# An encoder trunk on one core: one half of an early head pair kept on chip, earlier loads of attention's output, and projections run together in twelve heads

## The chip, the core and the metric

The kernel runs on one core of a Trainium2 chip. The metric is the device time of one execution in microseconds (us); lower is better. Five engines work side by side, each through its own list of instructions: TensorE (PE, matrix products into the accumulators of PSUM), VectorE (DVE), ScalarE (ACT), GpSimd (POOL), and SyncE (SP), which issues nearly all DMA transfers. An instruction that waits holds up everything behind it on its engine.

## What is computed

A trunk of two layers on one sequence of 1024 rows and 1024 columns in float32. Layer 0 has a gMLP mixer, layer 1 chunked attention with 16 heads of 64 columns; each is followed by a gated ConvFFN. What the change touches is the attention of layer 1 with the shared K and V, cut here to its core:

```python
kv = rmsnorm(h, kv_norm_g) @ w_kv                 # k and v for all heads
q = (h @ w_q).reshape(B, nc, CHUNK, N_HEADS, HEAD_DIM) * scale
def one_chunk(args):                              # 64 rows see their chunk and 8 before
    ...
    sc = jnp.einsum('bqhd,bkhd->bhqk', qb, kb).astype(jnp.float32) + bias
    sc = jnp.where(valid[None, None, None, :], sc, NEG_INF)
    p = jax.nn.softmax(sc, axis=-1).astype(vb.dtype)
    return jnp.einsum('bhqk,bkhd->bqhd', p, vb)
...
return o @ w_o
h = h + chunk_attention(rmsnorm(h, b_norm_g[j]), k_shared, v_shared, ...)
h = h + conv_ffn(rmsnorm(h, f_norm_g[l]), ...)
```

## The kernel before

**Numbers in two parts.** Every operand of a large product is split into a high part (a cast to the fast matmul type, on ACT, L138) and a low part (the rest, mostly on DVE, L139). A product is then three matmuls: high by high, high by low and low by high (L180, L183, L187). In the names, h and l at the end tell the part: `yh`, `yl`, `whi`, `wlo`, `ph`, `pl`, `vwh`, `vwl`, `oh`, `ol`.

**Before attention** `values()` computes V in Strassen-like products (matmuls L1174, sums `c` on DVE L1136). For the weights of the last products a DVE instruction at L1118 makes `vwl`. At its end `begin("q")` and `begin("k")` load the q and k weights of head pair 1; `put_off(us, fn)` runs `fn` after so many us of matmul work have been written, so that loading, scaling (POOL) and splitting (`whi`, `wlo`) are placed between the products.

**Attention** is one loop of 128 steps, `s = 8*hd + i`: head `hd`, key block `i`. A step writes, in this order:

- `head.score(i)`: scores of up to 5 query blocks against the key block (L1414 and L1416), a near tile of 256 columns and a far one (at `i = 4` one tile of 512). DVE adds the bias (L1420), ACT takes the exponentials (far L1424, near L1421) and casts to `ph` (L1427), POOL makes `pl` (L1428).
- fill products: matmuls of the q and k projections of later pairs, `n` of them, about 5.8 a step, one half here and the other half behind the values. From step `ends` = 104 (head 13) on the fill is the output projection `wo`.
- `mx.block(b)`: row maxima of the next head, a near block `mx` (L1229, DVE L1231) and a far one (L1235, DVE L1237). At a step they stand either in the middle (`mid`) or at the end (`end`). After step 5 the maxima are transposed (`mr`, L1252), copied by ACT, and a DMA writes them as one row of `qe`, which the next head's first score needs.
- `h0.value(b)`: probabilities by V of the step two before (L1444, L1446, L1448).

The tiles `st`, `mx` and `mr` share four PSUM banks, so that a new tile may wait for the reader of an older one.

**After a pair** p (two heads) and for each half t of the rows: ACT and DVE copy the product out (L1469, L1473), the sums of the softmax go through memory and come back as `den` (L1498), and `scale` divides (L1503), splits into the one buffer `oh`, `ol`, and `store` writes both to `osave` (L1512, L1513). `stays` marks a half that isn't stored but stays on chip in a place of `new_y()`. The output projection loads the stored halves with `load_o` (L1345, L1346), two transfers of 256 KB for one half of a pair. `load_hr` loads rows of the residual (L1574), `output_weight` the weights of `wo` (L1553), and `stage` copies q and k of the next head into place (L1215).

**What sets the order.** PE's instructions run in the order in which they are written. A scheduler sets the order on the other engines, SP's queue among them, and so decides which transfer is issued first.

Of the kernel before, what the change touches and what calls it, by code (L numbers as in the profile page):

```python
# [22 lines left out]
KD = D // P  # L23
# [23 lines left out]
def trunk(ctx: ExitStack, tc: tile.TileContext, x, a_win, a_wv, a_wst, a_bs, a_wout, w_kv, w_q, w_o,  # L47
# [1215 lines left out]
    with tc.tile_pool(name="vt", bufs=3, reuse_waits="tile") as vt, tc.tile_pool(name="vx", bufs=3, reuse_waits="tile") as vx, \  # L1263
# [16 lines left out]
        for t, _ in enumerate(values()):  # L1280
# [13 lines left out]
            if t:  # L1294
                def begin(what):
                    raw = new_raw([P, KD, P])
                    nc.sync.dma_start(raw, (w_q if what == "q" else w_kv)[1])
                    put_off(7.0, lambda: gains(what, raw))

                def gains(what, raw):  # L1300
                    c = C_BG if what == "q" else C_KVG
                    G.tensor_tensor(raw, raw, cc[:, c:c + KD].unsqueeze(2).broadcast_to([P, KD, P]), op=ALU.mult)
                    put_off(4.0, lambda: parted(what, raw))

                def parted(what, raw):
                    ws = [new_w() for _ in range(2)]
                    with tc.issue_after(behind[S].ins):
                        for i in range(2):
                            split(*ws[i], raw.rearrange("p k c -> p (k c)")[:, halves[i]])
                    w1[what] = tuple(Halves(t) for t in zip(*ws))  # L1310
                put_off(9.0, lambda: begin("q"))
                put_off(21.0, lambda: begin("k"))
                put_off(8.0, first_max)
# [35 lines left out]
    with tc.tile_pool(name="b1", bufs=1, reuse_waits="tile") as b1, \  # L1349
# [103 lines left out]
        class Pair:  # L1453
# [6 lines left out]
            def done(self, c, t, po):  # L1460
# [16 lines left out]
                stays = t == 0 and p >= LAST - 1  # L1477
# [40 lines left out]
                waits = (8.0, 8.0) if stays else (8.5, 8.0) if p == LAST - 1 else (10.5, 13.5 if p == LAST - 2 and t == 0 else 9.0)  # L1518
# [50 lines left out]
        def load_hr(i):  # L1569
            place = f32(bt.tile([P, T], F32R, tag=("thi", "tlo")[i % 2], name="hr"))  # L1570
            for j in range(2):
                hr[2 * i + j] = place[:, halves[j]]
                with tc.issue_after(behind["row"].ins):
                    nc.sync.dma_start(hr[2 * i + j], hsave[1][2 * i + j, :, halves[0]])  # L1574
# [3 lines left out]
        left = 2 * 6 * KD * LAST - early  # L1578
        ends = 13 * NB
        mid, end = {1: (1,), 2: (3,), 3: (5,), 4: (7,)}, {0: (0,), 1: (2,), 2: (4,), 3: (6,)}  # L1580
        for s in range(NH * NB):
# [11 lines left out]
            if s in (ends - 3, ends - 2, ends - 1, ends):  # L1593
                for k in ((0, 1), (2,), (3,), (4,))[s - ends + 3]:
                    load_o(k, 0)
# [7 lines left out]
            if s == ends + 6:  # L1603
                load_o(LAST - 2, 0)
# [21 lines left out]
            for _ in range(n // 2):  # L1626
                next(fill, None)
# [5 lines left out]
            if len(waiting) > LAG:  # L1633
                h0, b = waiting.pop(0)
                h0.value(b)
            for _ in range(n - n // 2):
                next(fill, None)
            if mx:
# [178 lines left out]
```

## Time and profile before

| | us |
|---|---|
| median of three runs | 2129.46 (2129.17 to 2131.74) |
| profiled execution | 2133.36 |
| its span in the trace | 2131.6 |
| attention's first score | at 1047.8 |
| head 13's first score | at 1342.06 |
| head 14's first score | at 1371.52 |

Times within the execution are counted from the start of the span. A row of the timeline gives the start, the duration, the engine with its source line, output and inputs, and in brackets how long the engine had been idle and what released it. A row of the view of waits sums such idle time by what was waited for, with the number of times and the longest. A row of the view of windows gives, for a stretch, each engine's busy time, PE's granted clock (PEclk, as a share of full speed), and what the DMA engines moved.

### The profile page before, as it was taken

What the parts mean: (1) busy time and instruction counts of PE and PEld (TensorE: products, weight loads), DVE (VectorE), ACT (ScalarE), POOL (GpSimd) and SP (SyncE); (2) the same over time, 40 slices, a digit from 0 to 9 for tenths busy, and PEclk for the clock granted to TensorE, in tenths of its full rate; (3) what the DMA queues carried; (4) which work ended last, traced back from release to release, by engine and by line L of the source; (5) the groups of instructions that cost most, each with busy time, mean ns of one, the idle gap of its engine ahead of it and who ended that gap; (6) DMA issues with size and microseconds to landing.
All of it is one profiled execution on the core that took longest, in us unless ns stands there. A gap on an engine that the chain in (4) does not pass through costs nothing.

```text
span 2131.6 us, 28895 instructions
## 1 busy us (share of the span) xinstructions
PE 2106.1 (99%) x9829; PEld 1758.3 (82%) x9829; DVE 1572.0 (74%) x2343; ACT 1086.2 (51%) x1896; POOL 790.0 (37%) x566
## 2 busy tenths in 40 slices
PE   9999999999999999999999999899999999999998
PEld 7888878888888888878888888788888888888887
DVE  5287789888888857776556666665988888885576
ACT  6533555554445544553466666653545544454443
POOL 1475744332334412042466655531322423342020
PEclk9999999999999999999999999999999999999999
DMA  7667722454445966734656566761244544478653
GB/s 255 194 243 261 238 99 100 138 187 142 169 164 195 330 226 221 263 101 143 187 132 167 140 157 162 197 216 62 72 152 136 183 139 172 164 274 309 211 189 129
DMA packets 205435, 384.63 MB, mean 180 GB/s; under 512 B 44388, under 2 KB 64204, under 8 KB 205288
## 3 DMA queue, kind: packets, MB, share of 16 engines
q1 hardware_dynamic: 201480, 376.88, 54.1%
q10 hardware_dynamic: 3808, 5.91, 0.8%
q8 instruction: 77, 1.26, 0.2%
q14 instruction: 70, 0.57, 0.1%
HBM read 247.28 MB, written 113.36 MB: 169 GB/s over the span
## 4 chain that ended last, share of the span: by engine, by line
PE 87%; DVE 6%; DMA 3%; issue 1%; ACT 1%; POOL 0%; SPq 0%; ACTq 0%; DVEq 0%; POOLq 0%
PE up L1044 10%; PE gate L1044 10%; PE up L368 7%; PE up L370 7%; PE up L373 7%; PE gate L373 6%; PE gate L368 5%; PE gate L370 5%; PE vps L520 4%; PE v L1174 3%; PE qkv L180 2%; PE qkv L183 2%; PE qkv L187 2%; PE ups L180 1%; PE ups L183 1%
## 5 line engine op out<-in xcount | busy, mean ns | idle before, releaser
L139 DVE TENSOR_TENSOR wlo<-raw,whi 128x512 fp32r<-128x512 f32 x376 | 332.1, 890 | 156.7 <-ACT whi L138 156.6
L138 ACT CAST whi<-raw 128x512 fp32r<-128x512 f32 x378 | 233.7, 620 | 269.6 <-PE gate L1044 194.4
L368 PE MATMUL up<-yh,whi 128*128 128x512 f32 x688 | 268.1, 390 | 0.5 <-ACT gate L930 0.5
L370 PE MATMUL up<-yh,wlo 128*128 128x512 f32 x688 | 268.0, 389 | 0.0
L891 POOL TENSOR_TENSOR h<-a 128x512 f32<-128x512 f32 x44 | 84.9, 1929 | 402.6 <-DVE a L883 390.0
L1428 POOL TENSOR_TENSOR pl<-p,ph 128x640 fp32r<-128x640 f32 (+4 forms) x128 | 159.0, 1245 | 146.8 <-ACT ph L1427 112.8
L368 PE MATMUL gate<-th,whi 128*128 128x512 f32 x496 | 193.1, 389 | 0.0
L370 PE MATMUL gate<-th,wlo 128*128 128x512 f32 x496 | 193.1, 389 | 0.0
L373 PE MATMUL up<-yl,whi 128*128 128x512 f32 x688 | 184.2, 389 | 0.0
L368 PEld LDWEIGHTS up<-yh,whi 128*128 128x128 f32 x688 | 129.2, 188 | 28.0 <-ACT gate L930 1.2
L373 PEld LDWEIGHTS up<-yl,whi 128*128 128x128 f32 x688 | 129.2, 188 | 27.2 <-POOL yl L139 0.5
L370 PEld LDWEIGHTS up<-yh,wlo 128*128 128x128 f32 x688 | 129.2, 188 | 26.6
L139 DVE TENSOR_TENSOR yl<-raw,yh 128x512 fp32r<-128x512 f32 x172 | 142.0, 827 | 8.1 <-ACT yh L138 8.1
L373 PE MATMUL gate<-tl,whi 128*128 128x512 f32 x496 | 132.8, 390 | 0.3 <-DVE tl L139 0.3
L138 ACT CAST whi<-S 128x512 fp32r<-128x512 f32 x160 | 99.1, 619 | 66.6 <-PE up L373 60.6
L139 DVE TENSOR_TENSOR wlo<-S,whi 128x512 fp32r<-128x512 f32 x160 | 130.2, 815 | 0.0
L1044 PE MATMUL up<-yl,whi 128*128 128x512 f32 (+1 forms) x312 | 120.8, 387 | 0.1
L1044 PE MATMUL up<-yh,wlo 128*128 128x512 f32 (+1 forms) x312 | 120.5, 386 | 0.2 <-DVE wlo L139 0.2
L1044 PE MATMUL up<-yh,whi 128*128 128x512 f32 (+1 forms) x312 | 120.5, 386 | 0.0
L1044 PE MATMUL gate<-yh,wlo 128*128 128x512 f32 (+1 forms) x312 | 120.4, 386 | 0.0
L1044 PE MATMUL gate<-yh,whi 128*128 128x512 f32 (+1 forms) x312 | 120.3, 385 | 0.0
L1044 PE MATMUL gate<-yl,whi 128*128 128x512 f32 (+1 forms) x312 | 120.2, 385 | 0.0
(452 smaller groups left out, 5397.9 us busy)
## 6 DMA issues: line engine op xcount, KB each, us to landing
raw<-in_f_win SPq DMA_DIRECT2D x88, 512.0 KB
gT<-h SPq DMA_DIRECT2D x88, 256.0 KB
h<-in_f_wdown SPq DMA_DIRECT2D x44, 512.0 KB
dS<-h SPq DMA_DIRECT2D x88, 256.0 KB
raw<-dS SPq DMA_DIRECT2D x40, 512.0 KB
raw<-gT SPq DMA_DIRECT2D x40, 512.0 KB
gB<-a SPq DMA_DIRECT2D x66, 256.0 KB
raw<-in_f_wdown SPq DMA_DIRECT2D x30, 512.0 KB
```

What stands on the lines that cost most here:

```text
L138: behind[S] = S.copy(hi, src)
L139: return eng.tensor_tensor(lo, src, f32(hi), op=ALU.subtract)
L180: nc.tensor.matmul(ps, wh[:, k, :], xs[k][0], start=k == first, stop=False)
L183: nc.tensor.matmul(ps, wl[:, k, :], xs[k][0], start=False, stop=False)
L368: nc.tensor.matmul(ps, wh[:, k, :], xs[k][0], start=first and k == 0, stop=False, skip_group_check=True)
L370: nc.tensor.matmul(ps, wl[:, k, :], xs[k][0], start=False, stop=False, skip_group_check=True)
L373: nc.tensor.matmul(ps, wh[:, k, :], xs[k][1], start=False, stop=k == 3, skip_group_check=True)
L520: nc.tensor.matmul(ps, a, b, start=k == i == 0, stop=k == KD - 1 and i == 2)
L891: G.tensor_tensor(B[n], x, B.get(y) if isinstance(y, str) else y, op=ALU.subtract)
L1044: nc.tensor.matmul(ps[:, cs], w[:, ms], x[:, cs], start=q == i == 0 and p in (1, 6, 5, 4), stop=q == NP - 1 and i == 2, skip_group_check=True)
L1174: nc.tensor.matmul(bank[m], a, b, start=p not in (2, 7) and k == i == 0, stop=k == 3 and i == 2, skip_group_check=True)
L1428: marks[2] = G.tensor_tensor(pl[:, :n], pf[:, :n], f32(ph[:, :n]), op=ALU.subtract)
```

## The change

1. `begin("k")` is put off by 25 us instead of 21.
2. `stays` holds for the first half (t = 0) of pair 5 too: it isn't stored in `osave` and isn't loaded again. The waits before `turned` and `scale` are adapted.
3. The places of the five loaded halves (pairs 0 to 4) are taken at step `ends - 3`, and all loads are written at steps `ends - 3` and `ends - 2`; before they were spread over four steps.
4. `load_hr` stays behind the last load of `o` where there is one, otherwise behind the last `row` DMA.
5. In the first twelve heads (`merged`) a step has another order: score, the end blocks of `mx` held over from the step before, value, mid blocks, and then all `n` fill products in one run.

```diff
-                put_off(21.0, lambda: begin("k"))
+                put_off(25.0, lambda: begin("k"))
...
-                stays = t == 0 and p >= LAST - 1
+                stays = t == 0 and p >= LAST - 2
...
-                waits = (8.0, 8.0) if stays else (8.5, 8.0) if p == LAST - 1 else (10.5, 13.5 if p == LAST - 2 and t == 0 else 9.0)
+                waits = ((8.5, 9.0) if t else (8.0, 8.0)) if p == LAST - 1 else (10.5, 13.5 if stays else 9.0)
...
-                with tc.issue_after(behind["row"].ins):
+                with tc.issue_after(behind["o"].ins if "o" in behind else behind["row"].ins):
                     nc.sync.dma_start(hr[2 * i + j], hsave[1][2 * i + j, :, halves[0]])
...
-        left = 2 * 6 * KD * LAST - early
+        left, held = 2 * 6 * KD * LAST - early, ()
...
-                for k in ((0, 1), (2,), (3,), (4,))[s - ends + 3]:
-                    load_o(k, 0)
+                if s == ends - 3:
+                    slots = [new_y() for _ in range(5)]
+                for k in ((0, 1), (2, 3, 4), (), ())[s - ends + 3]:
+                    load_o(k, 0, at=slots[k])
...
-            if s == ends + 6:
-                load_o(LAST - 2, 0)
...
-            for _ in range(n // 2):
-                next(fill, None)
+            merged = s < 12 * NB
+            for b in held:
+                mx.block(b)
+            held = []
+
+            def value():
+                if len(waiting) > LAG:
+                    h0, b = waiting.pop(0)
+                    h0.value(b)
+            if merged:
+                value()
+            else:
+                for _ in range(n // 2):
+                    next(fill, None)
             if hd + 1 < NH:
                 for b in mid.get(i, ()):
                     mx.block(b)
...
-            if len(waiting) > LAG:
-                h0, b = waiting.pop(0)
-                h0.value(b)
-            for _ in range(n - n // 2):
+            if not merged:
+                value()
+            for _ in range(n if merged else n - n // 2):
                 next(fill, None)
-            if mx:
+            if mx and merged:
+                held = end.get(i, ())
+            elif mx:
                 for b in end.get(i, ()):
                     mx.block(b)
```

What this does to the engines' lists is shown at three places. A row is the source line, the operation, its output and inputs with the buffers' numbers, the shape, and the engines or DMA queues that the instruction waits for.

**PE, head 2, step 4**, from the step's score on. Before, three projections (`qkv`) stand between the score and block 7 of the maxima (`mx`), and the values (`po`) follow:

```order
L1414 MATMUL st_10257<-qe0_8344,km0_8346 128x512 [waits DVE_49]
L1416 MATMUL st_10257<-qs0_8345,ks0_8343 128x512
L180 MATMUL qkv_10157<-yh_8541,whi_9730 128x512
L183 MATMUL qkv_10157<-yh_8541,wlo_9731 128x512
L180 MATMUL qkv_10157<-yh_8550,whi_9730 128x512
L1229 MATMUL mx_10270<-km1_9386,qe1_9384 128x256 [waits DVE_49]
L1235 MATMUL mx_10274<-km1_9386,qe1_9384 128x384 [waits DVE_49]
L1444 MATMUL po_10194<-ph_10180,vh0_9388 128x256
L1446 MATMUL po_10194<-ph_10180,vl0_9390 128x256
L1448 MATMUL po_10194<-pl_10181,vh0_9388 128x256 [waits Pool_49]
L1444 MATMUL po_10198<-ph_10180,vh0_9388 128x384
L1446 MATMUL po_10198<-ph_10180,vl0_9390 128x384
```

and with the change, the same step:

```order
L1414 MATMUL st_10250<-qe0_8344,km0_8346 128x512 [waits Activation_49]
L1416 MATMUL st_10250<-qs0_8345,ks0_8343 128x512
L1229 MATMUL mx_10260<-km1_9386,qe1_9384 128x256 [waits DVE_49]
L1235 MATMUL mx_10264<-km1_9386,qe1_9384 128x384 [waits DVE_49]
L1444 MATMUL po_10184<-ph_10173,vh0_9388 128x256
L1446 MATMUL po_10184<-ph_10173,vl0_9390 128x256
L1448 MATMUL po_10184<-pl_10174,vh0_9388 128x256 [waits Pool_49]
L1444 MATMUL po_10188<-ph_10173,vh0_9388 128x384
L1446 MATMUL po_10188<-ph_10173,vl0_9390 128x384
L1448 MATMUL po_10188<-pl_10174,vh0_9388 128x384
L1229 MATMUL mx_10273<-km1_9386,qe1_9384 128x256 [waits DVE_49]
L1235 MATMUL mx_10277<-km1_9386,qe1_9384 128x384 [waits DVE_49,Activation_49]
```

The two blocks of the step before (first `mx` pair) now stand right behind the score, the values ahead of block 7, and the projections behind all of it; the last row waits for ACT too, since its bank held the score `st` of the same step. Of the twelve merged heads the last row waits for ACT in six (2, 4, 6, 8, 10 and 11) and for DVE alone in the others.

**DVE, in `values()`, where the k weights of pair 1 are split** (`wlo`; `vwl` is the low part of a V weight, `c` a sum of the V products). Before:

```order
L1136 TENSOR_TENSOR c_9212<-v_9195,x_8391 128x512 [waits DMAHW3_49,DVE_49]
L139 TENSOR_TENSOR wlo_9240<-raw_9107,whi_9239 128x512 [waits Activation_49]
L139 TENSOR_TENSOR wlo_9242<-raw_9107,whi_9241 128x512 [waits Activation_49]
L1118 SCALAR_TENSOR_TENSOR vwl_9187<-raw_9185,cc_68,vwh_9186 128x512 [waits DMAHW0_49,Activation_49]
L1136 TENSOR_TENSOR c_9250<-v_9225,raw_8390 128x512 [waits DMAHW4_49,DVE_49,PE_49]
L1136 TENSOR_TENSOR c_9253<-v_9225,x_8391 128x512 [waits DMAHW5_49,DVE_49]
L1118 SCALAR_TENSOR_TENSOR vwl_9217<-raw_9215,cc_68,vwh_9216 128x512 [waits DMAHW1_49,Activation_49]
```

with the change:

```order
L1118 SCALAR_TENSOR_TENSOR vwl_9187<-raw_9185,cc_68,vwh_9186 128x512 [waits DMAHW0_49,Activation_49]
L1118 SCALAR_TENSOR_TENSOR vwl_9216<-raw_9214,cc_68,vwh_9215 128x512 [waits DMAHW1_49,Activation_49]
L1136 TENSOR_TENSOR c_9242<-v_9224,raw_8390 128x512 [waits DMAHW4_49,DVE_49,PE_49]
L1136 TENSOR_TENSOR c_9245<-v_9224,x_8391 128x512 [waits DMAHW5_49,DVE_49]
L139 TENSOR_TENSOR vtl_9257<-h10_83,vth_9256 128x512 [waits Activation_49]
L1136 TENSOR_TENSOR c_9273<-v_9260,raw_8389 128x512 [waits DMAHW6_49,DVE_49,PE_49]
L139 TENSOR_TENSOR wlo_9285<-raw_9148,whi_9284 128x512 [waits Activation_49]
L139 TENSOR_TENSOR wlo_9287<-raw_9148,whi_9286 128x512 [waits Activation_49]
```

The two splits of the k weights have moved from ahead of two `vwl` to six rows behind them.

**ACT and SP, pair 5's second half.** On ACT, in head 13's first steps, the cast of that half into `oh` (`oh`, the third row; the two ahead of it are exponentials of the step's scores). Before:

```order
L1424 ACTIVATE p_13435<-st_13441,cc_68 128x384 [waits PE_49,Pool_49]
L1421 ACTIVATE p_13435<-p_13435 128x256 [waits DVE_49]
L138 CAST oh_13159<-o_12867 128x512 [waits DMAHW7_49,DVE_49]
L1427 CAST ph_13445<-p_13435 128x640 [waits Activation_49]
L1424 ACTIVATE p_13473<-st_13479,cc_68 128x384 [waits PE_49,Pool_49]
```

with the change:

```order
L1424 ACTIVATE p_13433<-st_13439,cc_68 128x384 [waits PE_49,Pool_49]
L1421 ACTIVATE p_13433<-p_13433 128x256 [waits DVE_49]
L138 CAST oh_13157<-o_12860 128x512 [waits DVE_49]
L1427 CAST ph_13443<-p_13433 128x640 [waits Activation_49]
L1424 ACTIVATE p_13471<-st_13477,cc_68 128x384 [waits PE_49,Pool_49]
```

The cast no longer waits for a DMA queue; nothing else has moved there. On SP, ahead of head 13, the last rows up to the loads of `osave` and the transfers that bring the second half's sums (`rden51`, then `den`) and head 14's q and k (`qe0`, `km0`, `qs0`, `ks0`). Before:

```order
L1498 DMA den_12726<-rden50_9363 64x512 [waits DMAHW7_49,DMAHW6_49]
L1498 DMA den_12726<-rden50_9363 64x512
L1215 DMA qs0_8345<-thi_12962 64x512 [waits DMAHW0_49]
L1215 DMA km0_8346<-thi_13282 64x512 [waits DMAHW1_49,Activation_49]
L1215 DMA qs0_8345<-tlo_12963 64x512 [waits DMAHW2_49]
L1496 DMA rden51_9365<-few_13161 128x2x4 [waits DMAHW3_49,DVE_49]
L1215 DMA ks0_8343<-thi_13282 64x512 [waits DMAHW4_49]
L1215 DMA ks0_8343<-tlo_13283 64x512 [waits DMAHW5_49,DVE_49]
L1498 DMA den_12868<-rden51_9365 64x512 [waits DMAHW6_49,DMAHW3_49]
L1498 DMA den_12868<-rden51_9365 64x512 [waits DMAHW7_49]
L1346 DMA yl_13403<-osave_9341 128x512 [waits DMAHW0_49,PE_49]
L1346 DMA yl_13430<-osave_9341 128x512 [waits DMAHW1_49,PE_49]
```

with the change:

```order
L1345 DMA yh_13313<-osave_9341 128x512 [waits DMAHW7_49]
L1346 DMA yl_13314<-osave_9341 128x512 [waits DMAHW0_49,PE_49]
L1215 DMA qe0_8344<-thi_12962 64x512 [waits DMAHW1_49]
L1215 DMA km0_8346<-thi_13280 64x512 [waits DMAHW2_49,Activation_49]
L1215 DMA qs0_8345<-thi_12962 64x512 [waits DMAHW3_49]
L1496 DMA rden51_9365<-few_13159 128x2x4 [waits DMAHW4_49,DVE_49]
L1215 DMA qs0_8345<-tlo_12963 64x512 [waits DMAHW5_49]
L1215 DMA ks0_8343<-tlo_13281 64x512 [waits DMAHW6_49,DVE_49]
L1215 DMA ks0_8343<-thi_13280 64x512 [waits DMAHW7_49]
L1259 DMA bias_13572<-in_bias 128x256 [waits DMAHW0_49,DVE_49]
L1498 DMA den_12861<-rden51_9365 64x512 [waits DMAHW4_49,DMAHW1_49]
L1498 DMA den_12861<-rden51_9365 64x512 [waits DMAHW2_49]
```

Before, two of the ten loads of `osave` stood behind the second half's `den`; now all ten stand ahead of it, and the `den` of the first half (`den_12726` before) has moved ahead of nine of them, out of the rows shown.

## Prediction, on record before the changed kernel ran

> **What bounds the kernel now.** I read the page first, then PE's waits.
>
> ```profile
> PE 2106.1 (99%) x9829; PEld 1758.3 (82%) x9829; DVE 1572.0 (74%) x2343; ACT 1086.2 (51%) x1896; POOL 790.0 (37%) x566
> PE 87%; DVE 6%; DMA 3%; issue 1%; ACT 1%; POOL 0%; SPq 0%; ACTq 0%; DVEq 0%; POOLq 0%
> ```
>
> TensorE is busy for 2106.1 us of a span of 2131.6, and the change takes no matmul away. So it can gain only from PE's 25.5 us of idle time, and from what a slower clock behind an idle stretch costs. The waits say where:
>
> ```profile
> PE st L1414 <- DVE mb L1231: 8.0, 2, 7.8
> PE v L1174 <- DVE vwl L1118: 1.9, 2, 1.0
> PE st L1414 <- DMA qe<-mr: 1.1, 3, 0.5
> PE po L1448 <- POOL pl L1428: 0.9, 1, 0.9
> PE po L1444 <- ACT ph L1427: 0.3, 1, 0.3
> ```
>
> One wait of 7.8 us stands out. The windows put it into head 13; the first row holds heads 0 to 12, the second head 13, the others are pieces of it:
>
> ```profile
> 1047.80:1342.00 294.20, 292.17 (x1586) 252.99 (x1585) 187.31 (x510) 188.55 (x397) 174.48 (x151) 1.00 0.60 152
> 1342.00:1371.50 29.50, 21.65 (x117) 19.06 (x117) 16.47 (x42) 16.46 (x36) 14.17 (x13) 0.88 0.74 219
> ...
> 1350.00:1352.00 2.00, 0.00 (x0) 0.00 (x0) 0.00 (x0) 0.00 (x0) 0.00 (x0) 0.61 0.84 257
> 1352.00:1354.00 2.00, 0.00 (x0) 0.00 (x0) 0.76 (x2) 1.72 (x4) 0.40 (x1) 0.50 0.53 132
> 1354.00:1356.00 2.00, 1.67 (x6) 1.57 (x7) 1.68 (x7) 1.75 (x5) 1.61 (x2) 0.50 0.94 291
> 1356.00:1358.00 2.00, 2.00 (x10) 1.73 (x9) 1.02 (x4) 1.48 (x3) 1.71 (x2) 0.69 0.96 247
> ```
>
> Heads 0 to 12 leave PE only 2.03 us idle in 294; head 13 leaves 7.85 in 29.5. Behind its stall the granted clock is 0.50 until about 1357.3, while PE works from 1354.34 on: 3 us at half speed, 1.5 us lost. The same windows (0.61, 0.69) put the half clock from 1350.4 to 1357.2, so it came 4 us after PE went idle. Head 13's stall is worth **9.4 us** in all.
>
> **The change, part by part.** *Pair 5's first half stays (change 2).* The stall, followed back:
>
> ```profile
> 1346.27 0.22 PE L1235 MATMUL mx<-km,qe 128*128 128x128 f32 x1
> 1354.34 0.58 PE L1414 MATMUL st<-qe,km 128*128 128x256 f32 x1 [7.85 <-DVE mb L1231]
> 1353.24 0.69 DVE L139 TENSOR_TENSOR ol<-o,oh 128x512 fp32r<-128x512 f32 x1 [7.32 <-DMA osave<-ol]
> 1352.28 0.62 ACT L138 CAST oh<-o 128x512 fp32r<-128x512 f32 x1 [7.14 <-DMA osave<-oh]
> 1344.43 0.33 SPq L1512 DMA_DIRECT2D osave<-oh x1
> 1345.56 0.67 SPq L1513 DMA_DIRECT2D osave<-ol x1
> ```
>
> The score waits for DVE's `mb`, which stands behind `ol`, which waits with ACT's `oh` for the one buffer `oh`, `ol`: the store of pair 5's first half, issued at 1344.43 and 1345.56, must have left it. With the change this store doesn't exist, and the cast waits for DVE alone. What is late next is the second half's own sums:
>
> ```profile
> 1343.71 1.07 DVE L1503 TENSOR_TENSOR o<-o,den 128x512 f32<-128x512 f32 x1 [0.66 <-DMA den<-rden]
> 1345.51 0.41 DVE L1420 TENSOR_TENSOR p<-st,bias 128x256 f32<-128x256 f32 x1
> 1353.85 0.42 DVE L1231 CUSTOM_DVE_ANT_0 junk<-mx,bias 128x256 f32<-128x256 f32 x1
> 1339.90 1.10 SPq L1498 DMA_DIRECT2D den<-rden x2
> 1341.09 1.01 SPq L1346 DMA_DIRECT2D yl<-osave x2
> 1332.00:1336.00 4.00, 4.00 (x24) 3.59 (x23) 4.00 (x9) 2.31 (x6) 1.57 (x2) 1.00 0.99 262
> 1336.00:1340.00 4.00, 4.00 (x25) 3.15 (x23) 1.59 (x3) 1.63 (x5) 2.38 (x4) 1.00 0.77 170
> ```
>
> Were `den` as early as before, DVE would be free at 1345.92, make `ol` (0.69) and `mb` (0.42), and release the score at 1347.0, 0.5 us after PE came to it at 1346.49. But the two `yl` loads that were issued behind `den` now stand ahead of it (change 3): 0.5 MB, at the 170 to 262 GB/s of these windows 2.0 to 3.1 us. `den` had 0.66 us of wait already, but part of the extra falls where the queue idled, so I take 1.2 to 2.4 us more for DVE, and a stall of 1.7 to 2.9 us that remains, 2.0 as the value. Then 5.9 us of idle time go, and 1.5 of half clock, since such a stall ends before the 4 us are over. For a wait of head 14's first maxima on `km0`, which is issued behind the same ten loads, I take 0.9 off. **Head 13: −6.5 us**; bounds −3 (a stall of some 5 us stays, with its half clock) and −9.
>
> The Trainium skill, "TensorE: Matmul & The Clock Gate", Part 1 (the HAM clock gate), has the clock fall to half after an idle window of about 3.4 us, and return after about 3.4 us of work. The trace agrees: the half clock came after 4 us of idle time and ended 3 us after work came back. By this rule a stall of 2 us costs no half clock, and the sum stays; were the clock lost in proportion to the stall, 0.4 us of the 1.5 would stay and the sum be −9.1 instead of −9.5.
>
> No longer loading that half at `ends + 6` gives PE nothing by itself, since the first use of any loaded half is at step 104 or later and no wait on `yh` or `yl` stands among PE's waits. Its split keeps its work on ACT and DVE, into another place; that place is free, as no wait is added there. Change 4 moves residual loads by a few us, which are used long after.
>
> *The end of attention.* The second half of pair 6 has the same pattern, smaller:
>
> ```profile
> 1395.55 0.69 DVE L1503 TENSOR_TENSOR o<-o,den 128x512 f32<-128x512 f32 x1 [2.32 <-DMA den<-rden]
> 1397.58 0.49 PE L1444 MATMUL po<-ph,vh 128*128 128x512 f32 x1 [0.35 <-ACT ph L1427]
> 1399.24 0.50 PE L1448 MATMUL po<-pl,vh 128*128 128x512 f32 x1 [0.93 <-POOL pl L1428]
> ```
>
> DVE waits 2.32 us for `den` with the next bias add behind it, and PE pays 0.35 and 0.93 us two steps later, with some 0.2 for each restart of its pipeline. With `waits` of (8.5, 9.0) the multiplication stands behind that bias add and its cast behind `ph`. **−1.7 us**, bounds 0 and −1.9.
>
> *The k weights (change 1).*
>
> ```profile
> 1020.72 1.28 DVE L139 TENSOR_TENSOR wlo<-raw,whi 128x512 fp32r<-128x512 f32 x2
> 1021.92 0.74 DVE L1118 SCALAR_TENSOR_TENSOR vwl<-raw,cc,vwh 128x512 fp32r<-128x512 f32 x1
> 1023.78 0.74 DVE L1118 SCALAR_TENSOR_TENSOR vwl<-raw,cc,vwh 128x512 fp32r<-128x512 f32 x1
> ```
>
> Two `wlo`, 1.28 us, stand ahead of the two `vwl` for which PE waits 1.9 us. Now both `vwl` come first, the second ahead of two `c` of 0.6 us as well. **−1.8 us**, bounds −1 and −1.9. The k weights are about 5 us later; the 48 products of q in front of their first use (0.23 us each, 11 us) cover that.
>
> *The merged steps (change 5).* The same matmuls in another order; the price is what they wait for. A step as before, head 4, step 4:
>
> ```profile
> 1149.06 0.39 PE L1414 MATMUL st<-qe,km 128*128 128x512 f32 x1
> 1149.29 0.40 PE L1416 MATMUL st<-qs,ks 128*128 128x512 f32 x1
> 1149.91 0.41 DVE L1420 TENSOR_TENSOR p<-st,bias 128x256 f32<-128x256 f32 x1
> 1150.36 0.42 ACT L1421 ACTIVATE p<-p 128x256 f32<-128x256 f32 x1 [2.24 <-DVE p L1420]
> 1150.68 0.46 ACT L1424 ACTIVATE p<-st,cc 128x256 f32<-128x256 f32 x1
> ```
>
> Here is a new wait: with the change block 7's far matmul takes the bank of this step's score in six heads, and the far exponential (L1424) must have read it. That ends at 1151.14, 1.85 us after the second score matmul began. In the merged order PE would come to it 1.5 us after that, when the other bank's two `mx` and the six values are through (0.23 for the score's rest, 0.12 and 0.18 for `mx`, 0.88 for the values, 0.12). So 0.35 us of stall, 0.4 with the restart: 2.4 us in six heads, and at 0.1 each 0.6 in the others, whose row waits for an earlier DVE instruction. Against it, the blocks of maxima no longer crowd at the end of one step and the start of the next. The 2.03 us of idle time in heads 0 to 12 bound what can be seen of this; start to start, the matmuls of heads 0 to 11 take 5.1 us more than their usual spacing, 3.8 of it at step 2, where DVE is late with a maximum every other head. I take 2.8 of the 3.8 as gained. The wait for `qe<-mr`, 1.1 us in three heads, I leave as it is: `mr` comes one product later (0.23 us), the copy on ACT that it shares the engine with comes sooner; between 0.9 lost and 1.1 gained. Values come half a step sooner, by 0.5 to 1.1 us; `pl` was ready 0.6 us or more before its first use in these heads, mostly 2 to 3, so this costs at most a few tenths. Sum 2.4 + 0.6 − 2.8 + 0.3: **+0.5 us**, bounds −4 (every gap gone, no new wait) and +6 (0.6 us in each of twelve heads, nothing gained but 1).
>
> **Sum:** −6.5 − 1.7 − 1.8 + 0.5 = −9.5 us. The profiled execution took 2133.36 us, and would take 2123.9. The median shown is 2129.46, 3.9 us below it; with the same difference, **2120.0**. If part of the stall belongs to the profiled execution alone, the gain is smaller.
>
> **The rivals.**
>
> *The transfers take the stall's place* (little gained). Ten loads in one block ahead of `den`, `km0` and the rest. For it: DMA moved 257 GB/s in the middle of the stall already (window 1350 to 1352), and SP issues in order. Against it: 1 MB of stores and loads is gone from this stretch and the next. If head 13 keeps its whole stall, −1.7 − 1.8 + 0.5 = −3: 2126.5. [...]
>
> *The new wait on the score's bank decides* (slower). Place: block 7 at step 4 of the twelve merged heads. Its price is 0.4 us where ACT is free; if ACT has a cast (0.62 us, as in the row of `oh`) or two ahead of the exponentials, it is 1.0 to 1.6, and the values of the next steps come late too. From 1.2 us in each head, 14.4 in all, it eats the 10 us gained elsewhere and 4.3 more: 2134 and above. Against it: in head 4 ACT had been idle for 2.24 us when its exponential came.
>
> *Merging costs half of that* (0.6 us in each head, 7.2 more than the sum has): 2127.
>
> *All gaps go* (much faster): head 13 −9.4, the two others −3.5, and −4 from heads 0 to 11, which gives −17: 2112.5. Against it stands `den`'s lateness.
>
> That the cast still waits for a store is ruled out by its row on ACT; the store of the first half is gone from SP.
>
> **How the numbers follow.** The sum has 0.67, its own range 2117 to 2123; the transfers in the stall's place 0.13; the bank wait as a decider 0.06; merging at half that 0.06; all gaps gone 0.08. A measurement of this kernel tells about 0.2% from no change, 4.3 us: faster is under 2125.2, slower over 2133.7. The sum and the case of all gaps are faster, and a small part of the transfers' case: 0.76. The rest of that case and of the half-priced merging is within 0.2%: 0.18. Slower is the bank wait: 0.06. The range leaves out that and most of the case of all gaps: **2115 to 2127**.
>
> **What would show it.** Right: PE's wait on `mb` in head 13 falls from 7.85 to 1.5 to 3 us, and the granted clock stays at 1.0; the two waits on `vwl` and those on `ph` and `pl` at the end are gone; the heads 0 to 11 take as long as before within 2 us, with a new wait of L1235 on ACT's far exponential at step 4. Wrong: a wait on `qe`, `km` or `den` of 5 us in head 13 or 14; heads of 23.5 us and more before it; or the half clock again.

## The result and the profile after

The changed kernel takes 2127.32 us (median of 22 runs), the kernel before, run beside it, 2130.8 us (22 runs): a ratio of **0.9983, 95% interval 0.9976 to 0.9990**, 3.5 us less. The forecast was 9.5 us less, and 2115 to 2127 us. The profiled execution took 2130.35 us, with a span of 2128.6 against 2131.6.

PE's waits in the changed kernel's profile (us in total, times, longest):

```profile
PE po L1448 <- POOL pl L1428: 2.4, 3, 1.7
PE po L1444 <- DVE o L1473: 2.2, 1, 2.2
PE mx L1229 <- DVE mb L1231: 1.4, 2, 1.1
PE mx L1229 <- DMA km<-thi: 1.4, 1, 1.4
PE st L1414 <- DVE mb L1231: 1.3, 2, 0.7
```

The 7.8 us of head 13 and the two waits on `vwl` are gone. In their place stand waits that the kernel before had not, or not so long; only the score's wait on `mb`, the last row, is in part a rest of the old one. By stage, from the first score of a head to that of another, the two profiles give:

| stage | before, us | after, us | difference | forecast |
|---|---|---|---|---|
| up to head 0's first score | 1047.87 | 1045.61 | −2.3 | −1.8 |
| heads 0 to 11 (merged) | 270.58 | 272.51 | +1.9 | +0.5 |
| head 13 | 29.46 | 24.02 | −5.4 | −6.5 |
| end of attention: steps 0 to 3 of head 15, up to their last values (L1448 at 1402.40, 1398.66) | 10.08 | 12.07 | +2.0 | −1.7 |

Heads 12 and 14 are unchanged within 0.05 us. The sum is −3.8; 0.7 us are lost elsewhere, behind these steps. The merged heads and the end of attention are furthest from their forecast. Each profile is one execution, though, and the same stages differ between executions, as the profiles of the experiments show.

**Head 13** after, first as a window, then DVE and SP at its start, then PE's three waits:

```profile
1341.70:1365.80 24.10, 20.98 (x118) 17.69 (x118) 15.21 (x41) 15.60 (x35) 13.80 (x13) 1.00 0.76 206
```

```profile
1345.42 0.69 DVE L1503 TENSOR_TENSOR o<-o,den 128x512 f32<-128x512 f32 x1 [2.75 <-DMA den<-rden]
...
1341.97 1.10 SPq L1498 DMA_DIRECT2D den<-rden x2
...
1346.98 0.38 PE L1229 MATMUL mx<-km,qe 128*128 128x256 f32 x1 [1.11 <-DVE mb L1231]
1348.26 0.39 PE L1414 MATMUL st<-qe,km 128*128 128x256 f32 x1 [0.62 <-DVE mb L1231]
1352.71 0.39 PE L1229 MATMUL mx<-km,qe 128*128 128x256 f32 x1 [1.40 <-DMA km<-thi]
```

No store is waited for any more and the clock stays at 1.00. What is left is what now comes late: `den`, for which DVE waits 2.75 us instead of 0.66, and `km` of head 14.

**The end of attention** after, on DVE, ACT, POOL and PE, and the granted clock behind it:

```profile
1390.11 2.08 DVE L1503 TENSOR_TENSOR o<-o,den 128x512 f32<-128x512 f32 x1
1390.08 1.56 POOL L1428 TENSOR_TENSOR pl<-p,ph 128x640 fp32r<-128x640 f32 x1 [0.77 <-ACT ph L1427]
1392.22 0.62 ACT L138 CAST oh<-o 128x512 fp32r<-128x512 f32 x1 [1.43 <-DVE o L1503]
1392.86 0.58 ACT L1472 COPY den<-po 64x512 f32<-64x512 f32 x1
1393.66 0.68 DVE L1473 COPY o<-po 64x512 f32<-64x512 f32 x1
1394.40 0.33 PE L1444 MATMUL po<-ph,vh 128*128 128x128 f32 x1 [2.19 <-DVE o L1473]
```

```profile
1394.00:1396.00 2.00, 1.60 (x8) 1.46 (x9) 1.73 (x2) 1.94 (x5) 1.55 (x1) 0.79 0.94 287
1396.00:1398.00 2.00, 2.00 (x8) 1.81 (x7) 1.77 (x3) 2.00 (x5) 1.56 (x1) 0.50 0.92 320
1398.00:1400.00 2.00, 2.00 (x11) 1.78 (x10) 1.04 (x2) 0.81 (x2) 1.03 (x1) 0.86 0.37 134
```

The multiplication L1503 stands later, as forecast, and no longer waits for `den`. But it now runs while POOL makes `pl`, and takes 2.08 us instead of 0.69. Behind it stand ACT's cast `oh`, DVE's `ol`, and then the copies L1472 and L1473 that free PE's bank `po`: PE waits 2.19 us for them, and the clock is at half for 3.4 us on top.

**Head 7**, a merged head. SP's order, POOL, and PE's longest wait there:

```profile
1206.38 0.39 SPq L1512 DMA_DIRECT2D osave<-oh x1
1206.87 0.38 SPq L1513 DMA_DIRECT2D osave<-ol x1
1207.35 0.43 SPq L1373 DMA_DIRECT2D vl<-vd x1
1208.48 0.35 SPq L155 DMA_DIRECT2D raw<-in_w_q x1
1216.83 1.90 POOL L158 TENSOR_TENSOR raw<-raw,cc 128x1024 f32<-128x1024 f32 x1 [4.29 <-DMA raw<-in_w_q]
1218.68 2.78 POOL L1428 TENSOR_TENSOR pl<-p,ph 128x640 fp32r<-128x640 f32 x2
1220.27 0.33 PE L1448 MATMUL po<-pl,vh 128*128 128x128 f32 x1 [1.66 <-POOL pl L1428]
```

and the same place in the kernel before:

```profile
1208.04 0.42 SPq L155 DMA_DIRECT2D raw<-in_w_q x1
1209.21 0.38 SPq L1373 DMA_DIRECT2D vl<-vd x1
1210.34 0.33 SPq L1512 DMA_DIRECT2D osave<-oh x1
1212.54 1.90 POOL L158 TENSOR_TENSOR raw<-raw,cc 128x1024 f32<-128x1024 f32 x1
```

All projections of a step now stand at its end, and so the weights for the next ones are asked for later, behind two stores of 256 KB and the load of `vl`. POOL multiplies them by the gain 8.35 us after the issue instead of 4.5, waits 4.29 us for them, and `pl` stands behind it. PE, which comes to the values sooner than before, waits for that.

### The profile page after: what moved, and what is told of

The parts are those of the page before. It is cut to its first block, busy times and chain, and to the rows that moved or that the text cites. A ratio compares the mean times of both kernels' runs of the same rounds, so it can differ in the third digit from the quotient of the medians.

```text
span 2128.6 us, 28878 instructions
## 1 busy us (share of the span) xinstructions
PE 2106.5 (99%) x9829; PEld 1759.2 (83%) x9829; DVE 1576.7 (74%) x2343; ACT 1087.6 (51%) x1896; POOL 790.5 (37%) x566
## 5 line engine op out<-in xcount | busy, mean ns | idle before, releaser
L1044 PE MATMUL up<-yl,whi 128*128 128x512 f32 (+1 forms) x312 | 120.8, 387 | 0.2
L1044 PE MATMUL up<-yh,wlo 128*128 128x512 f32 (+1 forms) x312 | 120.5, 386 | 0.2
L1044 PE MATMUL up<-yh,whi 128*128 128x512 f32 (+1 forms) x312 | 120.4, 386 | 0.0
L1044 PE MATMUL gate<-yh,wlo 128*128 128x512 f32 (+1 forms) x312 | 120.4, 386 | 0.0
L1044 PE MATMUL gate<-yh,whi 128*128 128x512 f32 (+1 forms) x312 | 120.2, 385 | 0.0
L1044 PE MATMUL gate<-yl,whi 128*128 128x512 f32 (+1 forms) x312 | 120.1, 385 | 0.0
```

The source lines that it names most:

```text
L1044: nc.tensor.matmul(ps[:, cs], w[:, ms], x[:, cs], start=q == i == 0 and p in (1, 6, 5, 4), stop=q == NP - 1 and i == 2, skip_group_check=True)
```

## The experiments

Ratios are to the kernel before, each with runs of it beside; medians are compared inside one group only (e1 to e4, e5 to e8, e9 to e12). "Heads 0 to 11" is the time from the first score of head 0 to that of head 12 in the profile.

### Without the merged steps (e1)

```diff
-            merged = s < 12 * NB
+            merged = False
```

> The change without its merged steps (part 5), all else kept. Theory A (the merged order itself costs: values come sooner and wait for POOL's pl behind its multiplication of the weights, 2.4 us of PE waits plus a half clock in head 7, against the gaps at step 2 that it removes): 2 to 4 us faster than the changed kernel, that is about 6 us (0.9970) faster than before, and in the profile heads 0 to 11 take 5 us over the usual spacing as before. Theory B (head 7's wait was an accident of the one profiled execution, a slow weight load; merging else gains): 0 to 3 us slower than the changed kernel, 0.5 to 3.5 us faster than before.

Measured: 0.9977 (0.9968 to 0.9986), 2126.99 us. Heads 0 to 11 take 270.05 us against 272.51 in the changed kernel, and no wait on `pl` stands there; the end of attention has the same 2.2 us. The gain over the changed kernel's 0.9983 lies inside the intervals, so the time alone doesn't settle it. This profile speaks for A, others in part for B. The profiles of e2, e3, e4 and e7 have the merged steps with the same order on SP in head 7, and heads 0 to 11 take 270.48, 268.83, 268.69 and 272.32 us there. PE's wait on `pl` in head 7 is 1.18 us in e2 and 2.17 in e7; in e3 and e4, where POOL waited 2.06 and 2.11 us for the weights instead of 4.29, PE doesn't wait. So what merging costs differs from one execution to the next: from 2.5 us more than in e1 to 1.4 less.

### The wait of 8.0 us for pair 6's second half (e2)

```diff
-                waits = ((8.5, 9.0) if t else (8.0, 8.0)) if p == LAST - 1 else (10.5, 13.5 if stays else 9.0)
+                waits = ((8.5, 8.0) if t else (8.0, 8.0)) if p == LAST - 1 else (10.5, 13.5 if stays else 9.0)
```

> The change with the wait of pair 6's second half put back from 9.0 to 8.0 us, so that its multiplication by the softmax sums (L1503) stands ahead of the second bias add of head 15 again. Theory A (the later place is what costs the 2.2 us wait on L1473 and the half clock behind it): that wait goes, den is there by 1388 in this kernel's time since no load of osave is under way, the stretch of head 15's steps 0 to 3 costs under 1 us, and the kernel is 3 us faster than the changed kernel, about 6.5 us faster than before. Theory B (den comes late there whatever the place, as in the kernel before): PE's waits on ph and pl of 1.3 us come back, and the kernel is at most 1.5 us faster than the changed one.

Measured: 0.9974 (0.9965 to 0.9983), 2126.69 us. DVE and PE at the end of attention:

```profile
1388.39 0.69 DVE L1503 TENSOR_TENSOR o<-o,den 128x512 f32<-128x512 f32 x1 [2.02 <-DMA den<-rden]
1392.08 0.50 PE L1448 MATMUL po<-pl,vh 128*128 128x512 f32 x1 [0.93 <-POOL pl L1428]
```

The wait on L1473 and the half clock are gone, as A says; `den` is as late as before (2.02 us, before 2.32), as B says, and 0.93 us of wait on `pl` come back. With POOL idle L1503 takes 0.69 us.

The four steps of the end of attention take 9.79 us, against 12.07 in the changed kernel. But 1.5 us of that difference is the half clock, which need not follow. Eight more kernels here have the later place (e1, e3, e4, e6, e7, e9, e10, e12), all with the same wait of 2.2 us on L1473; in seven of them no half clock follows, and the four steps take 10.51 to 10.65 us, against 10.08 before. Nor does the earlier place keep it away: in e8 the four steps take 12.17 us, with a half clock. So the later place is no gain: it costs 0.4 to 0.6 us, and 2.0 where the half clock follows it. Head 13 took 26.67 us in this profile, 2.7 more than in the changed kernel: DVE waited 4.58 us for `den` there, and 6.8 us of half clock followed.

### The loads of o spread as before (e3)

```diff
-                if s == ends - 3:
-                    slots = [new_y() for _ in range(5)]
-                for k in ((0, 1), (2, 3, 4), (), ())[s - ends + 3]:
-                    load_o(k, 0, at=slots[k])
+                for k in ((0, 1), (2,), (3,), (4,))[s - ends + 3]:
+                    load_o(k, 0)
```

> The change with the five loads of o spread over steps 101 to 104 as before; merged steps and all else kept. Theory A (the ten loads in one block delay den and km0 ahead of heads 13 and 14): the waits on mb (2.3 us) and on km (1.6 us) in head 13 fall to under 1.5 us together, and the kernel is 1.5 to 3 us faster than the changed one. Theory B (those transfers are late anyhow, or DVE's own order sets the wait on mb): head 13 keeps 3 us or more of waits, and the time is within 1 us of the changed kernel.

Measured: 0.9969 (0.9958 to 0.9980), 2125.47 us. PE's waits:

```profile
PE mx L1229 <- DMA km<-thi: 2.3, 1, 2.3
PE po L1444 <- DVE o L1473: 2.2, 1, 2.2
PE st L1414 <- DVE mb L1231: 0.6, 1, 0.6
PE mx L1229 <- DVE mb L1231: 0.3, 1, 0.3
```

In head 13 the waits on `mb` fell (one of those rows, 0.3, is head 12's), but the one on `km` grew to 2.3 us: the two theories are both half right. The stall moves between the transfers. Head 13 takes 25.60 us in this profile, with a half clock behind the wait on `km`, 1.6 more than in the changed kernel; so this profile doesn't explain the better median by head 13.

### The k weights at 21 us (e4)

```diff
-                put_off(25.0, lambda: begin("k"))
+                put_off(21.0, lambda: begin("k"))
```

> The change with the k weights begun at 21 us as before. The two waits on vwl (1.9 us) come back, with their restarts: 2 us slower than the changed kernel, 1.5 us faster than before. If the place of the k weights' split is hidden, no difference to the changed kernel.

Measured: 0.9986 (0.9976 to 0.9996), 2128.76 us. The row `vwl` is back with 1.9 us, and head 0 begins at 1046.98 instead of 1045.61. In the median the part can't be told from no difference. Head 13 has the same order here as in the changed kernel, but DVE waited 4.30 us for `den` in this execution, and PE lost a half clock behind it.

### The merged steps alone (e5)

The kernel before with the order of part 5, as in the diff of the change:

```diff
+            merged = s < 12 * NB
+            for b in held:
+                mx.block(b)
...
+            if merged:
+                value()
```

> The kernel before with the merged steps alone (part 5). Theory A (values that come sooner wait for POOL's pl, at head 3, head 5 and, where the weights come late, head 7; what is gained at step 2 is given back): heads 0 to 11 take 3 to 7 us over the usual spacing against 5 before, the profile shows waits of L1448 on pl of 1 us or more in sum, and the time is within 1.5 us of before. Theory B (merging gains the gaps of heads 0 to 11, and the changed kernel's waits came from the other parts): 2 to 4 us faster than before, no wait on pl there.

Measured: 1.0005 (0.9992 to 1.0017), 2133.94 us; the profiled execution was the slowest of its runs. Heads 0 to 11 take 273.29 us, against 270.58 before, and PE's waits have this row:

```profile
PE po L1448 <- POOL pl L1428: 3.8, 3, 2.6
```

2.6 us of it are in head 7, 0.3 in head 5, 0.9 at the end of attention. Merging alone shows no gain: the interval leaves out B's 2 to 4 us.

### Values behind half of the projections (e6)

```diff
+            for _ in range(n // 2):
+                next(fill, None)
             if merged:
                 value()
-            else:
-                for _ in range(n // 2):
-                    next(fill, None)
...
-            for _ in range(n if merged else n - n // 2):
+            for _ in range(n - n // 2):
```

> The change with the merged steps in another order: score, the held blocks, half of the projections, then values, middle blocks and the other half. Values come 0.5 to 0.7 us later than in the change. Theory A (it is the earlier values that wait for pl): the waits on pl in heads 3, 5 and 7 go or fall under 0.3 us each, the far block of step 4 no longer waits for ACT, heads 0 to 11 take under 3 us over the usual spacing, and the kernel is 2 us faster than the changed one. Theory B (POOL is late whatever the order): the waits on pl stay, no difference.

Measured: 0.9991 (0.9977 to 1.0005), 2130.06 us, which can't be told from no difference. The waits on `pl` in heads 5 and 7 and that of the far block of step 4 went, but head 3's grew:

```profile
PE po L1444 <- DVE o L1473: 3.6, 5, 2.2
PE st L1414 <- DMA qe<-mr: 2.0, 3, 0.9
PE po L1448 <- POOL pl L1428: 1.5, 1, 1.5
```

and four waits on L1473 inside the merged heads and three on `qe` came with it. Heads 0 to 11 take 273.15 us. A fails as it was put: later values alone don't help, since other waits take their place. And in head 7 it isn't the later values that helped. With half of the projections ahead of them the weight load is issued ahead of the stores again, and POOL doesn't wait for it:

```profile
1205.79 0.38 SPq L155 DMA_DIRECT2D raw<-in_w_q x1
1207.10 0.38 SPq L1373 DMA_DIRECT2D vl<-vd x1
1208.35 0.33 SPq L1512 DMA_DIRECT2D osave<-oh x1
1210.54 1.91 POOL L158 TENSOR_TENSOR raw<-raw,cc 128x1024 f32<-128x1024 f32 x1
```

That is 4.75 us from issue to multiplication, as in the kernel before: it is the load's place on SP that decides in head 7.

### The low parts behind den (e7)

```diff
-                for k in ((0, 1), (2, 3, 4), (), ())[s - ends + 3]:
-                    load_o(k, 0, at=slots[k])
+                for k in ((0, 1, 2, 3, 4), (), (), ())[s - ends + 3]:
+                    os_[0][k] = slots[k]
+                    behind["o"] = nc.sync.dma_start(f32(slots[k][0]), osave[0, k, :, halves[0]])
+                for k in ((), (), (0, 1, 2, 3, 4), ())[s - ends + 3]:
+                    behind["o"] = nc.sync.dma_start(f32(slots[k][1]), osave[1, k, :, halves[0]])
```

> The change with the five loads of the high parts of o at step ends - 3 and those of the low parts only at ends - 1, so that the second half's den stands ahead of the low parts on SP. Theory A (the loads ahead of den set the wait on mb): DVE's wait for den in head 13 falls from 2.8 to under 1.2 us, and PE's waits on mb there to 1 us or less; the transfers behind, km of head 14 or the low parts themselves, come later, so that a wait of 2 to 5 us on them is new and the time is about that of the changed kernel, within 2 us. Theory B (den is late for another reason): DVE's wait for den stays at 2 us or more.

Measured: 0.9967 (0.9953 to 0.9981), 2125.85 us. DVE's wait for `den`, and PE's wait on `km`:

```profile
1340.90 0.69 DVE L1503 TENSOR_TENSOR o<-o,den 128x512 f32<-128x512 f32 x1 [0.29 <-DMA den<-rden]
```

```profile
PE mx L1229 <- DMA km<-thi: 3.0, 1, 3.0
```

With five loads ahead of `den` instead of ten its wait falls from 2.75 to 0.29 us, and `km`, now behind the low parts, is 3.0 us late. That is theory A: it is the loads in front that decide when `den` comes. Head 13 as a whole gains nothing by it in this profile: it takes 25.12 us, with a half clock behind the wait on `km`.

### Kept half, k weights, spread loads and 8.0 us together (e8)

The edits of e1, e2 and e3 on the change:

```diff
+            merged = False
...
+                waits = ((8.5, 8.0) if t else (8.0, 8.0)) if p == LAST - 1 else (10.5, 13.5 if stays else 9.0)
...
+                for k in ((0, 1), (2,), (3,), (4,))[s - ends + 3]:
+                    load_o(k, 0)
```

> The parts that gained, together: pair 5's half kept on chip and the k weights later, without the merged steps, with the loads of o spread as before and with the wait of 8.0 us for pair 6's second half. If the gains add (e1, e2 and e3 each alone are 1.3 to 2.9 us faster than the changed kernel), 9 us faster than before, 0.9958. If they are not independent (the transfers ahead of head 13 settle the same stall), 6 us, 0.9970. In the profile head 13's waits should be under 3 us, those at the end of attention 1 us.

Measured: 0.9974 (0.9960 to 0.9987), 2127.93 us: the gains don't add. Head 13 takes 21.83 us (1338.64 to 1360.47), 2.2 less than in the changed kernel, but ACT's `ph` is 1.0 us late at the end of attention beside 0.9 us on `pl`, with a half clock, and PE loses some 2 us more behind attention. 0.9 us of that is a wait for `wlo` in a product of the last ConvFFN (L1044); what delays it there wasn't followed.

### The gain left out, merged (e9) and not (e10)

In both the q and k weights of pairs 2 to 7 aren't multiplied by the norm's gain, so that POOL waits for no weights.

```diff
-                nw = w1["k"] if n == 0 else weights(*order[n + 1]) if n + 1 < len(order) else None
+                nw = w1["k"] if n == 0 else load_w((w_q if order[n + 1][1] == "q" else w_kv)[order[n + 1][0]]) if n + 1 < len(order) else None
```

> The change, and POOL's multiplication of the q and k weights by the norm's gain is left out for pairs 2 to 7, so that POOL waits for no weight load in attention. Theory A (values wait for pl because pl stands on POOL behind that multiplication, which waits for weights that SP now issues behind the stores of o): all waits on pl in heads 3 to 7 go, heads 0 to 11 take 2 to 4 us over the usual spacing (the six waits of 0.3 us at step 4 and the DMA of the row maxima stay), about 3 us less than in the changed kernel. Theory B (pl is late because ACT's ph or DVE are late): the waits on pl stay at 1 us or more in sum.

> The same with the gain left out, without the merged steps. This is the pair to e9: the difference of the two is what merging is worth when POOL isn't in its way. Theory A (merging gains the gaps at step 2): e9 is 2 to 3 us faster than this one, heads 0 to 11 here 4 to 5 us over the usual spacing. Theory B (merging is worth nothing in any case): the two are within 1 us.

Measured: 0.9971 (0.9960 to 0.9981) merged, 0.9978 (0.9969 to 0.9986) not merged. Windows of 266 us over these heads, PE's busy time second: first the changed kernel, then e9, then e10.

```profile
1046.00:1312.00 266.00, 262.14 (x1425) 228.86 (x1424) 173.54 (x467) 171.35 (x357) 159.55 (x136) 0.99 0.58 149
```

```profile
1046.00:1312.00 266.00, 265.19 (x1450) 232.17 (x1449) 174.00 (x470) 174.45 (x366) 145.67 (x131) 1.00 0.60 150
```

```profile
1046.00:1312.00 266.00, 264.43 (x1436) 229.29 (x1435) 170.33 (x469) 171.37 (x362) 143.02 (x128) 1.00 0.58 148
```

With this work of POOL's gone, PE does 1450 matmuls in the time in which it did 1425, no wait on `pl` is left, and heads 0 to 11 take 267.34 us against 270.08 unmerged, 2.7 us less. 1.1 us of the 2.7 are two waits in head 10 that e10 has in this execution (0.33 on `mb`, 0.80 on `qe`). The medians, 2125.67 and 2127.02 us, go the same way, but their intervals overlap. The profiles speak for A in both: merging can gain up to 2.7 us net. With POOL's multiplication in place the merged heads take 1.5 and 1.4 us longer in e3 and e4, and 5.2 in the changed kernel.

### The low parts behind head 14's copies (e11)

The edits of e1 and e2, and:

```diff
-                for k in ((0, 1), (2, 3, 4), (), ())[s - ends + 3]:
-                    load_o(k, 0, at=slots[k])
+                for k in ((0, 1, 2, 3, 4), (), (), ())[s - ends + 3]:
+                    os_[0][k] = slots[k]
+                    behind["o"] = nc.sync.dma_start(f32(slots[k][0]), osave[0, k, :, halves[0]])
...
                     stage(hd + 1, halves[1])
+                if s == ends:
+                    for k in range(5):
+                        behind["o"] = nc.sync.dma_start(f32(slots[k][1]), osave[1, k, :, halves[0]])
```

> A version meant to be faster: pair 5's half on chip and the k weights later, no merged steps, 8.0 us for pair 6's second half, the high parts of o loaded at step ends - 3 and the low parts only at step ends, behind the copies of head 14's q and k. If the loads ahead of den and km are what is left in head 13, its waits on mb and km fall under 1.5 us together, no wait on the low parts comes in their place (they are first used eleven products into head 13), and the kernel is 7 to 9 us faster than before, 0.9962. If the low parts land late, a wait on them of 1 to 4 us shows in head 13 and the time is that of e2, 0.9974.

Measured: **0.9956 (0.9945 to 0.9968), 2121.56 us** against 2131.47 of the kernel before beside it: faster than both kernels. Head 13 as a window:

```profile
1338.60:1358.90 20.30, 20.21 (x118) 17.80 (x117) 15.83 (x40) 15.48 (x35) 14.44 (x13) 1.00 0.93 261
```

It takes 20.25 us instead of 29.46, and PE is idle for 0.09. The DMA engines are busier than before (0.93 of the time, against 0.74). On SP all five low parts now stand behind the second half's `den`, three of them ahead of head 14's `km` and two behind it.

### Pair 5's half kept, alone (e12)

The kernel before with part 2 alone, its 9.0 us for pair 6 included; loads and residual rows as before:

```diff
-                stays = t == 0 and p >= LAST - 1
+                stays = t == 0 and p >= LAST - 2
...
-                waits = (8.0, 8.0) if stays else (8.5, 8.0) if p == LAST - 1 else (10.5, 13.5 if p == LAST - 2 and t == 0 else 9.0)
+                waits = ((8.5, 9.0) if t else (8.0, 8.0)) if p == LAST - 1 else (10.5, 13.5 if stays else 9.0)
...
-            if s == ends + 6:
-                load_o(LAST - 2, 0)
```

> The kernel before with pair 5's first half kept on chip alone (part 2 with its 9.0 us for pair 6's second half); the k weights, the loads and the steps as before. Theory A (the parts act in their own stages): vwl's 1.9 us stay, head 13 keeps 3 to 4 us of waits, the end of attention waits 2.2 us for L1473: 3 to 4 us faster than before, 0.9983. Theory B (the loads in one block are needed for the gain): no faster than before within 1 us.

Measured: 1.0013 (1.0004 to 1.0021), 2134.64 us: slower, which neither theory gave. The profiled execution was the fastest of its runs (2129.31 us) and shows a wait that no other kernel has:

```profile
PE wo L180 <- DMA yh<-osave: 1.6, 1, 1.6
```

SP issued the last two high parts behind residual rows and a weight load, 0.2 us before head 13's first score, and PE waited for them. Head 13 takes 24.04 us all the same, as in the changed kernel. What makes the other runs slower stays open. It isn't the spread loads as such, since e3 and e8 keep the half with spread loads and are faster than before. They also have change 4, and there these residual rows are issued behind the last loads of `o`; e12 leaves it out. And this profile loses 4.0 us more than the one of the kernel before behind the end of attention, with waits of 1.7 and 0.6 us in the last ConvFFN (L1044). Whether either loss grows in the longer runs was not seen.

## Why the prediction was wrong

Between the two profiles the gain is 3.0 us instead of 9.5. The miss of 6.5 us is made up of 3.7 at the end of attention, 1.4 in the merged heads, 1.1 in head 13 and 0.7 behind attention, less 0.5 that the k weights gained beyond their term.

- **What bounds the kernel** and where its idle time lay were read rightly: the stages that moved are those that the prediction named, but for 0.7 us behind attention.
- **The k weights**, −1.8: right, −2.3 in the profile; e4 brings the 1.9 us of waits back.
- **Head 13**, −6.5: the mechanism was right, the term mis-sized. The store's 7.85 us went. `den` became late by 2.1 us more, inside the forecast 1.2 to 2.4, and `km` cost 1.4 instead of 0.9, so the profile has −5.4. But that was one execution. In the seven profiles with all ten loads ahead of it on SP (the changed kernel, e1, e2, e4, e6, e9, e10) DVE waited 1.70 to 4.88 us for `den`, and head 13 took 2.8 to 6.4 us less than before: the value was set at the good end. With five or six loads ahead (e3, e7, e8, e11, e12) the wait was 0 to 1.48 us. e11 shows that with the low parts behind `den` the whole 9.2 us can be had; e7, with them behind `den` but all ahead of `km`, shows the stall move to `km`.
- **The end of attention**, −1.7: the step failed, and with its sign. It looked at what the later place frees (the bias add) and not at what stands behind the moved multiplication: `oh` and `ol`, then L1472 and L1473, for which PE waits 2.2 us. And it took 0.69 us for an instruction that takes 2.08 beside POOL's `pl`. Measured +2.0, of which 1.5 is the half clock, and +0.4 to +0.6 in the seven profiles of other kernels where none follows; in e2, with the earlier place, the wait on L1473 is gone.
- **The merged steps**, +0.5: the mechanisms were seen, but not their sizes, and one was missed. The new wait at step 4 shows as 0.27 to 0.29 us in the six named heads, 1.7 in all instead of 2.4, and the other six heads have none. Without POOL's work the net was −2.7 (e9 against e10). What failed is "Values come half a step sooner … so this costs at most a few tenths". The slack of `pl` was read from the kernel before, where POOL multiplied the weights 4.5 us after their issue. The change moves that load behind 768 KB on SP and so `pl`, by some 4 us in head 7. Of the moved steps the DMAs were counted for `den`, not for the weights. The result, +1.9 in the changed kernel's profile, was between −1.9 and +1.7 in e2, e3, e4 and e7: that the forecast lies between them is luck, since it gave this wait 0.3 us.
- **The clock**: "since such a stall ends before the 4 us are over" failed. It held in head 13 of the changed kernel, but stalls of 1.66 and 2.19 us elsewhere were each followed by a half clock of 3.4 us, 1.5 us lost each time. The Trainium skill, "TensorE: Matmul & The Clock Gate", Part 1, has the clock fall after an idle window of about 3.4 us; these rows show it after 1.66 us, and the measurement decides.
- **The loads sooner and the residual rows later** (changes 3 and 4), nothing: open. In head 13 the loads in one block are what makes `den` late. e12, which leaves both changes out, is slower than before, but what makes it so wasn't shown.
- **Behind attention**, nothing: 0.7 us more than before in the changed kernel's profile, 0.1 to 4.0 in the others. Why is open.
- The rival of the transfers that take the stall's place came nearest: it had 2126.5 us, with 0.13. Its mechanism fits only in part: the transfers left 3.1 us of waits in head 13, not the whole stall, and the rest of the miss lies in other stages.

## What to carry to other kernels

When instructions move, list the DMAs that move with them and what each of them is now behind on its queue: three of the surprises here were transfers (`den`, `km`, the weights) that the new order put behind bulk loads or stores. Measure the slack of a buffer in the order in which it will be used, since it includes what its producer waits for. And put bulk transfers behind the small ones that somebody waits for: nearly the same bytes in another order took head 13 from 24.02 us in the changed kernel to 20.25 in e11. And read a stage in more than one execution before a wait in it is given a price: here the same order of instructions gave waits for `den` of 1.70 to 4.88 us.

## What the runs showed of the hardware

- The half clock comes in pieces of 3.41 us or a multiple, whose starts in one execution lie on one grid: in the changed kernel at 1221.07 and 1395.15 us, 51 times 3.413 apart. It followed idle times as short as 1.66 us (head 7) and 0.97 and 0.95 close together (e8), and didn't follow 2.18 us in e1 or 2.17 in e7. So the same stall costs 1.5 us more or nothing. What decides was not shown: the wait of 2.2 us on L1473 was followed by a half clock in two of nine profiles, and in these two all or nearly all of it lay inside one piece of the grid, while in the seven others two pieces shared it; but shorter stalls inside one piece brought it in some places and not in others.
- DVE's L1503 took 2.08 or 2.09 us in all nine profiles that have it at the later place, and 0.69 in the five that have it at the earlier one, with POOL idle. At the later place POOL's `pl` had begun 0.03 us earlier in the changed kernel, and L1503 ended 0.55 us after it. So it did elsewhere: at 1378.27 us of the changed kernel L1503 took 1.02 us, with the last 0.48 us of a `pl` beside it, and in e7 1.04 us beside 0.49. A `pl` that began after it cost it nothing (e7 at 1340.90, 0.69 us). A DVE instruction beside POOL is not priced by its mean.
